# A hybrid S5 and attention layer on one core: the norm of x on VectorE, a pinned order from the u products on, the keys' norms a tile behind, and block 0's output matrices and lags behind the keys

## The chip, the cores and the metric

The kernel runs on one core of a Trainium2 chip. The metric is the device time of one execution in microseconds, shown as the median of three runs. Five engines work at the same time, each through its own queue in order: TensorE (PE in the profile; PEld is its weight load), VectorE (DVE), ScalarE (ACT), GpSimd (POOL) and SyncE (SP), which issues all the transfers here. Engines wait for one another by semaphores.

## What is computed

One layer of a diffusion backbone, on 512 latent tokens x and 256 context tokens ctx of width 1024, conditioned by a vector c. Cut to what the change touches:

```
mod    = silu(c) @ w_mod + b_mod            # 6 vectors of 1024; another set from c_ctx for ctx
h      = rmsnorm(x, norm1)   * (1 + sc1)  + sh1
hc     = rmsnorm(ctx, norm1) * (1 + csc1) + csh1
q, k, v, u, g = split(h @ w_in)             # ctx: k, v, u alone
k      = rope(rmsnorm(k));  kc = rmsnorm(kc)     # two key heads of 128
y      = s5(u, uc)                          # scan over the tokens, both directions, 32 groups of 64 complex states
attn   = softmax(q [kc, k]^T / sqrt(128)) [vc, v]
x      = x + g1 * ((sig(ga) * (attn @ w_ab) + sig(gs) * glu(gelu(y))) @ w_out)
x      = x + g2 * conv_ffn(rmsnorm(x, norm2) * (1 + sc2) + sh2);  out = rmsnorm(x)
```

The S5 scan is worked in chunks of 8 tokens: input matrices W (from B and powers of the step A), output matrices H (from C), the products inside a chunk ("lags", from H, C and W), and a scan over the chunks.

## The kernel before, in words

Every matrix product takes three TensorE products (`mm3`, L129), because weights and activations are split into a high and a low part: ScalarE casts the high part, and the low part is the remainder, by GpSimd for weights (`split`, L134, L136) and by VectorE for activations. Weights come through three staging buffers `wr` and two pairs `wh`, `wl` (`weight`, L138). PSUM has four single banks ("a") and two double ones ("s").

The head of the program, in the order of the code:

1. Constants, x, the first modulation weights (`load_wm`, two buffers in each of two tags, 1 MB each for one of eight tiles) and ctx are asked for on SP. VectorE and ScalarE work out the S5 step: sines, powers, the tables `ws`, `hs`, `wa`, `wb` (L244 to L329).
2. `rstd_first` (L350): for x, ScalarE squares each of eight tiles and TensorE adds up all eight with a product by ones; for ctx, VectorE adds the squares and TensorE multiplies only the sum and the last square. Then logarithm and exponential give the reciprocal root.
3. For each of eight tiles k (L408): the modulation sums of tile k+1 (`mod_sums`: eight products with a 32-column left side, a copy of the row by VectorE), the turning of tile k's row into columns (`mod_turn`, `finish`), then h for x and ctx (scaling on VectorE L416, shift on ScalarE L417, remainder on VectorE L418), and the u products: `ul` (latent, 512 wide) and `uc` (context, 256 wide), 12 of each.
4. u goes to DRAM and back in another layout (`ub`, `ud`, `us`). `s5_build(0)` makes W, the padded copies of it on ScalarE (L493), and H on VectorE, twelve passes of 128x1024.
5. `keys` (L660): for two heads, a tile for ctx and one for the latents: 24 products `kp`, ScalarE's square, a ones product `kss` for the sum, rotary products on VectorE, reciprocal root, scaling, split.
6. `s5_lags(0)`: products `kps`, a copy and a correction on VectorE, a store to DRAM and eight loads back as `tp`. `turn` makes the rotation tables of a half block.
7. The S5 stage (L785): four blocks in two halves. `weave` interleaves VectorE's `s5_half` with TensorE's steps; `filler` hands out value tiles `vp`, gates `proj` and the rest of the modulation in small pieces, so TensorE has work while VectorE scans. `s5_out` closes a half.

What sets the order: the framework schedules instructions by their dependences and its own estimate of times; `nosync` adds an order without a wait. From L783 on (`pinned[0] = True`) each TensorE instruction is tied behind the one before it in the code; ahead of it the scheduler mixes tiles as it sees fit. `behind` (L229, L418) holds the S5 products `tt` back behind the latest remainder of h.

Of the kernel before, what the change touches and what calls it, by code (L numbers as in the profile page):

```python
# [18 lines left out]
KT = 8  # L19
L = 512  # L20
# [9 lines left out]
LOADS = "xxwcw"  # L30
WU_V = ()
PO2 = 2
GAP, F0, F1, F2, F3, WM = 2, 8, 13, 5, 2, 2
PO3 = 0
# [28 lines left out]
def hybrid_layer_kernel(ctx: ExitStack, tc: tile.TileContext, io, out):  # L63
# [56 lines left out]
    def pe(ins):  # L120

        if pinned[0]:
            nosync(ins, last[0])
        last[0] = ins
# [67 lines left out]
    x = [None] * 8  # L192
    cx = k8("y8", [KT, LC])
    i = 0
    for what in LOADS:
        if what == "x":
            xt = k8("x8", [4, L])
            S.dma_start(xt, io["x"][:, 4 * i:4 * i + 4])
            x[4 * i:4 * i + 4] = [xt[:, j] for j in range(4)]
            i += 1  # L200
        elif what == "c":
            S.dma_start(cx, io["ctx"])
            S.dma_start(sd, io["sd"])
        else:
            load_wm()
# [23 lines left out]
    behind = [None]  # L229

    def tt(o, a, b, op, eng=V):
        i = eng.tensor_tensor(o, a, b, op=op).ins  # L232
        if behind[0] is not None:
            nosync(i, behind[0])
# [17 lines left out]
    z1, z2, ang8 = sm("n"), sm("n2"), sm("a8")  # L252
    r1, r8 = sm("r1"), sm("r8")
    wrap(ang, r1, z1)
    V.tensor_scalar(r1, r1, PI_LO, -PI_LO, op0=OP.min, op1=OP.max)
    table("silu_and_others")
    sn, co, ab = sm("sn"), sm("co"), sm("ab")
    act(sn, r1, AF.Sin)
    A.activation(ab, r1, AF.Abs)
    act(co, ab, AF.Sin, scale=-1.0, bias=half_pi)  # L260
    V.tensor_scalar(ang8, ang, float(TC), None, op0=OP.mult)
    wrap(ang8, r8, z2)
    fr, fhi, flo = sm("fr"), sm("fhi"), sm("flo")
    V.tensor_scalar(fr, r8, 1.0 / TWO_PI, None, op0=OP.mult)
    V.tensor_scalar(fhi, fr, 192.0, None, op0=OP.add)
    V.tensor_scalar(fhi, fhi, 192.0, None, op0=OP.subtract)
    tt(flo, fr, fhi, OP.subtract)

    pw = tz([8, 2, 32], "tab", 2)
    pf = tz([8, 2, 32], "tab", 2)  # L270
    tt(pw[:, 0, 0], mag, co, OP.mult)
    tt(pw[:, 0, 1], mag, sn, OP.mult)

    def cmul(o, a, b, n):

        c1, c2 = tz([8, 32], "bb", 2)[:, 0:n], tz([8, 32], "bb", 2)[:, 0:n]
        br, bi = (b[:, None, i].to_broadcast([128, n, 32]) for i in range(2))
        tt(c1, a[:, :, 0], br, OP.mult)
        tt(c2, a[:, :, 1], bi, OP.mult)
        tt(o[:, :, 0], c1, c2, OP.subtract)  # L280
        tt(c1, a[:, :, 0], bi, OP.mult)
        tt(c2, a[:, :, 1], br, OP.mult)
        tt(o[:, :, 1], c1, c2, OP.add)

    cmul(pw[:, 1:2], pw[:, 0:1], pw[:, 0], 1)
    cmul(pw[:, 2:4], pw[:, 0:2], pw[:, 1], 2)
    cmul(pw[:, 4:8], pw[:, 0:4], pw[:, 3], 4)
    den, nr, c1, c2 = sm("den"), sm("nr"), sm("c1"), sm("c2")
    tt(c1, lr, lr, OP.mult)
    tt(c2, li, li, OP.mult)  # L290
    tt(den, c1, c2, OP.add)
    V.reciprocal(den, den)
    V.tensor_scalar(nr, pw[:, 0, 0], 1.0, None, op0=OP.subtract)
    ni = pw[:, 0, 1]
    tt(c1, nr, lr, OP.mult)
    tt(c2, ni, li, OP.mult)
    tt(c1, c1, c2, OP.add)
    tt(pf[:, 0, 0], c1, den, OP.mult)
    tt(c1, ni, lr, OP.mult)
    tt(c2, nr, li, OP.mult)  # L300
    tt(c1, c1, c2, OP.subtract)
    tt(pf[:, 0, 1], c1, den, OP.mult)
    cmul(pf[:, 1:8], pw[:, 0:7], pf[:, 0], 7)

    ws, hs = tz([2, 32, 8], "ws"), tz([2, 32, 8], "hs")
    for o, i, up in ((ws, pf, 0), (hs, pw, 0)):
# [873 lines left out]
```

## Time and profile before

| what | us |
|---|---|
| median of three runs (978.12 to 981.64) | 979.43 |
| the profiled execution | 978.9 |
| its span, from the first to the last instruction | 976.8 |
| busy in it: TensorE / VectorE / ScalarE / GpSimd | 920.1 / 495.2 / 416.8 / 364.5 |

The mean granted clock of TensorE is 0.977 of its full speed. The span is cut into 40 slices of 24.4 us below; a digit is the busy share of a slice in tenths. The head of the program is the first five slices:

```profile
PE   5897889999978999999999999999999999999996
DVE  6559799595417777777434553433333333200103
ACT  7324644344364445544533443444434444432332
POOL 1124132332323222222246420665555655554552
PEclk9998989999998999999999999999999999999998
```

A busy TensorE is not one at its peak: each matmul is recorded with its latency, and neighbours overlap. The time a product really takes is the distance from its start to the next start. Idle time of an engine that is not the bound costs nothing.

### The profile page before, as it was taken

What the parts mean: (1) busy time and instruction counts of PE and PEld (TensorE: products, weight loads), DVE (VectorE), ACT (ScalarE), POOL (GpSimd) and SP (SyncE); (2) the same over time, 40 slices, a digit from 0 to 9 for tenths busy, and PEclk for the clock granted to TensorE, in tenths of its full rate; (3) what the DMA queues carried; (4) which work ended last, traced back from release to release, by engine and by line L of the source; (5) the groups of instructions that cost most, each with busy time, mean ns of one, the idle gap of its engine ahead of it and who ended that gap; (6) DMA issues with size and microseconds to landing.
All of it is one profiled execution on the core that took longest, in us unless ns stands there. A gap on an engine that the chain in (4) does not pass through costs nothing.

```text
span 976.8 us, 15643 instructions
## 1 busy us (share of the span) xinstructions
PE 920.1 (94%) x6142; PEld 741.7 (76%) x6142; DVE 495.2 (51%) x935; ACT 416.8 (43%) x795; POOL 364.5 (37%) x282
## 2 busy tenths in 40 slices
PE   5897889999978999999999999999999999999996
PEld 2676767676657888888778989888888888888886
DVE  6559799595417777777434553433333333200103
ACT  7324644344364445544533443444434444432332
POOL 1124132332323222222246420665555655554552
PEclk9998989999998999999999999999999999999998
DMA  9616546565522111111124620333233233333332
GB/s 358 227 47 190 151 142 185 168 194 179 168 80 77 39 49 44 44 44 45 44 65 140 204 67 1 108 96 98 87 98 98 86 100 95 88 102 93 97 108 87
DMA packets 56377, 107.24 MB, mean 110 GB/s; under 512 B 6000, under 2 KB 19056, under 8 KB 54640
## 3 DMA queue, kind: packets, MB, share of 16 engines
q1 hardware_dynamic: 56304, 106.25, 34.7%
q8 instruction: 48, 0.79, 0.3%
q14 instruction: 25, 0.20, 0.1%
HBM read 101.02 MB, written 5.21 MB: 109 GB/s over the span
## 4 chain that ended last, share of the span: by engine, by line
PE 73%; DVE 10%; ACT 5%; issue 5%; DMA 2%; POOL 1%; DVEq 0%; ACTq 0%; POOLq 0%
PE up L127 25%; PE down L127 12%; PE proj L127 10%; PE po L127 6%; PE sc L127 3%; PE glu L127 3%; PE pab L127 3%; DMA wr<-wo 2%; PE tps L901 2%; PE ul L127 2%; DVE w L232 2%; DVE t L232 2%; DVE k L232 1%; PE kp L127 1%; ACT wh L135 1%
## 5 line engine op out<-in xcount | busy, mean ns | idle before, releaser
L136 POOL TENSOR_TENSOR wl<-wr,wh 128x512 fp32r<-128x512 f32 x226 | 312.3, 1401 | 570.0 <-ACT wh L135 563.2
L127 PE MATMUL up<-t,wh 128*128 128x512 f32 (+1 forms) x768 | 225.2, 377 | 1.1 <-DVE t L1018 1.0
L135 ACT CAST wh<-wr 128x512 fp32r<-128x512 f32 x226 | 128.0, 609 | 119.1 <-PE down L127 40.5
L127 PEld LDWEIGHTS up<-t,wh 128*128 128x128 f32 x768 | 139.9, 188 | 31.3 <-DVE t L1018 2.3
L127 PE MATMUL up<-t,wl 128*128 128x512 f32 (+1 forms) x384 | 144.7, 377 | 0.0
L127 PE MATMUL proj<-h,wh 128*128 128x512 f32 x384 | 141.2, 422 | 0.0
L127 PEld LDWEIGHTS proj<-h,wh 128*128 128x128 f32 x384 | 74.8, 195 | 21.6 <-issue 6.1
L127 PEld LDWEIGHTS up<-t,wl 128*128 128x128 f32 x384 | 72.2, 188 | 14.6
L127 PE MATMUL proj<-h,wl 128*128 128x512 f32 x192 | 77.6, 404 | 2.7 <-POOL wl L136 2.7
L1052 DVE SCALAR_TENSOR_TENSOR zc<-up,pv,zc 128x511 f32<-128x511 f32 x44 | 33.0, 750 | 88.3 <-ACT zc L1051 88.3
L1051 ACT ACTIVATE zc<-up,pv 128x512 f32<-128x512 f32 x44 | 34.2, 777 | 75.0 <-PE up L127 74.9
L1083 DVE SCALAR_TENSOR_TENSOR x<-down,mods,x 128x512 f32<-128x512 f32 (+1 forms) x9 | 6.2, 692 | 91.0 <-PE down L127 91.0
L135 ACT CAST pth<-tps 128x512 fp32r<-128x512 f32 x48 | 28.1, 586 | 47.7 <-PE tps L901 47.5
L127 PEld LDWEIGHTS proj<-h,wl 128*128 128x128 f32 x192 | 37.6, 196 | 8.8 <-POOL wl L136 3.1
L127 PE MATMUL glu<-w,wh 128*128 128x512 f32 x128 | 42.5, 393 | 0.0
L889 DVE TENSOR_REDUCE sc<-sc 128x1 f32<-128x768 f32 x32 | 30.7, 961 | 21.8 <-PE sc L127 21.7
L136 DVE TENSOR_TENSOR ptl<-tps,pth 128x512 fp32r<-128x512 f32 x48 | 33.0, 688 | 13.5 <-ACT pth L135 13.2
L127 PE MATMUL sc<-g,qh 128*128 128x256 f32 (+1 forms) x128 | 36.6, 339 | 0.0
L127 PE MATMUL down<-h,wh 128*128 128x512 f32 x112 | 35.6, 389 | 0.0
L127 PE MATMUL po<-pth,g 128*128 128x512 f32 x96 | 32.9, 423 | 1.0 <-ACT pth L135 0.6
L1053 DVE SCALAR_TENSOR_TENSOR zc<-up,pv,zc 128x511 f32<-128x511 f32 x44 | 33.0, 750 | 1.6
L108 ACT ACTIVATE P<-sc,nb,rq 128x768 f32<-128x768 f32 x32 | 31.9, 997 | 4.1 <-DVE nb L890 2.4
(292 smaller groups left out, 1730.9 us busy)
## 6 DMA issues: line engine op xcount, KB each, us to landing
wr<-wup SPq DMA_DIRECT2D x88, 256.0 KB, 2.7
wm<-wmB SPq DMA_DIRECT2D x32, 512.0 KB, 4.8
wr<-wdn SPq DMA_DIRECT2D x40, 256.0 KB, 2.7
x<-x SPq DMA_DIRECT2D x4, 1024.0 KB, 5.3
g<-wmA SPq DMA_DIRECT2D x4, 1024.0 KB, 8.4
w<-wmA SPq DMA_DIRECT2D x4, 1024.0 KB, 10.1
wr<-wgs SPq DMA_DIRECT2D x16, 256.0 KB, 3.5
wr<-wga SPq DMA_DIRECT2D x16, 256.0 KB, 2.7
```

Source lines behind the costliest of these rows:

```text
L108: i = A.activation(*a, **k).ins
L127: pe(T.matmul(ps, l, r, start=start, stop=stop).ins)
L135: A.copy(hi, src)
L136: eng.tensor_tensor(lo, src, f(hi), op=OP.subtract)
L232: i = eng.tensor_tensor(o, a, b, op=op).ins
L889: V.tensor_reduce(mx, sv, axis=AX.X, op=OP.max)
L901: pe(T.transpose(tps[:, 128 * b:128 * b + 128], Ps[h][b][:, 128 * j:128 * j + 128], ident).ins)
L1051: A.activation(z, ps, AF.Identity, scale=cw[1], bias=pv[:, PV_CB + i:PV_CB + i + 1])
L1052: V.scalar_tensor_tensor(z[:, 1:512], ps[:, 0:511], cw[0], z[:, 1:512], op0=OP.mult, op1=OP.add)
L1053: V.scalar_tensor_tensor(z[:, 0:511], ps[:, 1:512], cw[2], z[:, 0:511], op0=OP.mult, op1=OP.add)
L1083: V.scalar_tensor_tensor(x1[i][:, c], ps[:, c], g2[:, i:i + 1], x1[i][:, c], op0=OP.mult, op1=OP.add)
```

## The change

Its parts:

- **Norm of x.** `rstd_first` always adds the squares on VectorE; TensorE multiplies the sum and the last square. The norm of ctx is moved behind the first tile's u products.
- **S5 step spread.** The table work of step 1 becomes a generator, `discretised`; the entry `DISC[k]` says how many of its pieces are issued with tile k (the last entry, 4, before the norm of x). The tables `wa` and `wb` come last.
- **Order from u on.** TensorE's order is pinned from the start to the end of the u products. In each tile: turn k+1, scale x of k+1 and ctx of k, the latent products of k, the modulation sums of k+2, the context products of k-1. The row of sums is copied by ScalarE, not by VectorE. Loads: both x, then modulation and u weights in turn, ctx after two of the modulation tiles; u weights come in pairs of tiles (`wu` has another layout in DRAM).
- **Keys.** A tile's sum of squares and all behind it (`normed`) is issued inside the next tile's products, after four k of a latent tile or six of a context tile. `keys` yields after each tile, and the rest of `s5_build(0)` (the second half: H, after six steps of W) stands between its two heads.
- **Lags.** `s5_lags(0)` goes from ahead of the S5 stage into its first `weave`, with nine more steps there; the first two steps of `s5_drive(0, 0)` come ahead of the last key's norm.

```
-LOADS = "xxwcw"
+DISC = 1, 2, 2, 2, 2, 2, 2, 0, 4
...
-    rs_x = rstd_first(lambda k: x[k], L, True)
-    rs_c = rstd_first(lambda k: cx[:, k], LC, False)
+    table("silu_and_others")
+    extra = discretised()
+    steps(extra, DISC[KT])
+    table("natural_log_exp_and_others")
+    rs_x = rstd_first(lambda k: x[k], L)
...
+    mod_sums(0)
+    mod_turn(0)
+    scaled(x[0], rs_x, hh[0], 0, 0)
+    low(x[0], hh[0], hl[0], 0, 0)
+    mod_sums(1)
+    for k in range(KT):
+        if k + 1 < KT:
+            mod_turn(k + 1)
+            scaled(x[k + 1], rs_x, hh[k + 1], k + 1, 0)
+            if k:
+                scaled(cx[:, k], rs_c, ch[:, k], k, 1)
+            low(x[k + 1], hh[k + 1], hl[k + 1], k + 1, 0)
+        elif k:
+            scaled(cx[:, k], rs_c, ch[:, k], k, 1)
+        u_of(k, False)
+        if k == 0:
+            rs_c = rstd_first(lambda k: cx[:, k], LC)
+            uc = [bank("uc") for _ in range(2)]
+            scaled(cx[:, 0], rs_c, ch[:, 0], 0, 1)
+        low(cx[:, k], ch[:, k], cl[:, k], k, 1)
+        steps(extra, DISC[k])
+        mod_sums(k + 2)
+        if k:
+            u_of(k - 1, True)
+        if k in (2, 4):
+            wus.append(weight(io["wu"][k // 2 + 1], [2, 512]))
+    u_of(KT - 1, True)
+    run(extra)
+    pinned[0] = False
...
-    run(s5_build(0))
-    behind[0] = None
+    hold[0] = behind[0]
+    first = s5_build(0)
+    steps(first, 6)
+    hold[0] = None
...
     s5_u(0)
-    keys()
-    run(s5_lags(0))
-    run(turn(0))
-    run(turn(1))
+    pinned[0] = True
+    kg = keys()
+    steps(kg, 2)
+    run(first)
+    steps(kg, 2)
...
-    pinned[0] = True
-    run(s5_drive(0, 0))
+    d00 = s5_drive(0, 0)
+    steps(d00, 2)
+    run(kg)
+    run(turn(0))
+    run(turn(1))
+    run(d00)
...
-        weave(s5_half(s, 0), chain(s5_drive(s, 1), fill), 8, 6 + F0)
+        weave(s5_half(s, 0), chain(s5_drive(s, 1), s5_lags(0) if s == 0 else (), fill), 8, 6 + F0 + (9 if s == 0 else 0))
```

**What moves, at three places.** First TensorE from its first instruction to the first u products (`n`: ones products of the norms, `mod`: modulation sums and turnings, `ul`: u products). Before:

```order
L358 MATMUL n_203<-tg,ones 128x512 x8
L127 MATMUL n_231<-p,ones 128x256
L127 MATMUL n_231<-tg,ones 128x256
L378 MATMUL mod<-g_86,cz 32x256 x8
L378 MATMUL mod<-g_90,cz 32x256 x8
L383 MATMUL mod<-cst,bb 32x2 x16
L127 MATMUL ul<-h_263,wh 128x512
```

and now:

```order
L126 MATMUL n_156<-p,ones 128x512
L126 MATMUL n_156<-tg,ones 128x512
L399 MATMUL mod<-g_85,cz 32x256 x8
L404 MATMUL mod<-cst,vr 32x2 x8
L399 MATMUL mod<-g_97,cz 32x256 x8
L404 MATMUL mod<-cst,vr 32x2 x8
L126 MATMUL ul<-h_188,wh 128x512
```

Eight ones products of the norm of x have become two, and the two of the context's norm have gone behind the first tile.

Second TensorE at the end of a head's context keys and the start of its latent ones (`kp`: key products, `kss`: the sum of squares). Before, at the second head:

```order
L127 MATMUL kp<-c_267,wl 128x256
L127 MATMUL kp<-c_268,wh 128x256
L127 MATMUL kss<-tg,ones 128x256
L127 MATMUL kp<-h_263,wh 128x512
L127 MATMUL kp<-h_263,wl 128x512
L127 MATMUL kp<-h_265,wh 128x512
```

and now, within the latent tile of the first head:

```order
L126 MATMUL kp<-h_188,wh 128x512
L126 MATMUL kp<-h_188,wl 128x512
L126 MATMUL kp<-h_190,wh 128x512
L126 MATMUL kss<-tg,ones 128x256
L126 MATMUL kp<-h_189,wh 128x512
L126 MATMUL kp<-h_189,wl 128x512
```

The sum of the context tile, which stood right behind its products, now stands behind twelve products of the next tile.

Third SP at block 0's lags (`ldr`: the store, `tp`: the eight loads back, `wm`: modulation weights, `wr`: staged weights). Before:

```order
L147 DMA wr<-wgs 128x512 x2
L514 DMA ldr<-lg 128x240
L517 DMA tp<-ldr 16x8x128 x8
L732 DMA wm<-wmB 128x1024 x2
L483 DMA bb<-sb 128x256
```

and now:

```order
L531 DMA bb<-sc 128x256
L561 DMA ldr<-lg 128x240
L792 DMA wm<-wmB 128x1024 x2
L564 DMA tp<-ldr 16x8x128 x8
L792 DMA wm<-wmB 128x1024 x2
```

Two modulation loads now stand between the store of the lags and the loads that bring them back.

## Rows read from the trace of the kernel before

**Rows 1.** Windows of core 0, whole head and S5 stage: us, busy by engine, PEclk, DMA share, GB/s:

```profile
0.00:28.43 28.43, 15.00 (x84) 6.82 (x85) 18.63 (x89) 19.94 (x40) 2.63 (x15) 0.94 0.91 346
28.43:76.51 48.08, 45.50 (x384) 35.39 (x385) 28.91 (x53) 14.61 (x27) 13.23 (x9) 0.97 0.35 121
76.51:106.71 30.20, 23.11 (x106) 17.96 (x105) 23.05 (x26) 14.69 (x32) 8.34 (x6) 0.89 0.73 221
106.71:141.00 34.29, 31.36 (x410) 27.44 (x409) 33.44 (x60) 17.69 (x42) 3.90 (x3) 0.95 0.37 106
141.00:283.00 142.00, 134.88 (x1592) 97.10 (x1591) 90.63 (x153) 56.79 (x138) 45.03 (x28) 0.98 0.56 175
```

**Rows 2.** Timeline of TensorE, 0 to 30: start us, us, engine line op, count, idle before and releaser:

```profile
8.65 10.07 PE L358 MATMUL n<-tg,ones 128*128 128x512 f32 x16 [8.65 <-ACT tg L357]
...
23.62 2.52 PE L378 MATMUL mod<-g,cz 128*32 128x256 f32 x32
...
28.43 0.79 PE L127 MATMUL ul<-h,wh 128*128 128x512 f32 x1 [1.43 <-ACT h L417]
```

**Rows 3.** Timeline of ScalarE, 18 to 22:

```profile
18.52 0.62 ACT L309 COPY ws<-tab 128x256 f32<-128x256 f32 x1
...
19.59 0.67 ACT L108 ACTIVATE tp<-n,cc 128x512 f32<-128x512 f32 x1
20.18 1.01 ACT L339 ACTIVATE tg<-y 128x256 f32<-128x256 f32 x3
21.09 0.61 ACT L108 ACTIVATE tp<-tp 128x512 f32<-128x512 f32 x1
```

**Rows 4.** Waits of TensorE to 110 (total, times, longest), and its timeline at 84:

```profile
PE kss L127 <- ACT tg L670: 7.1, 4, 4.5
...
84.04 1.22 PE L127 MATMUL kss<-tg,ones 128*128 128x256 f32 x2 [4.49 <-ACT tg L670]
```

**Rows 5.** Timeline of ScalarE, at 83:

```profile
82.95 0.63 ACT L493 ACTIVATE wpad<-k 64x128 f32<-64x128 f32 x2 [4.53 <-DVE k L232]
```

**Rows 6.** Timeline of VectorE, at 9 and 109:

```profile
8.91 0.35 DVE L232 TENSOR_TENSOR bb<-tab 128x64 f32<-128x64 f32 x2
...
109.36 0.69 DVE L679 TENSOR_TENSOR tg<-tg 128x512 f32<-128x512 f32 x1
```

**Rows 7.** Timelines of VectorE and GpSimd, at 70:

```profile
69.43 1.22 DVE L232 TENSOR_TENSOR k<-bb,ws 128x1024 f32<-128x1024 f32 x1
70.57 2.31 DVE L232 TENSOR_TENSOR t<-bb,ws 128x1024 f32<-128x1024 f32 x1
...
69.99 1.81 POOL L136 TENSOR_TENSOR wl<-wr,wh 128x512 fp32r<-128x512 f32 x1 [8.04 <-ACT wh L135]
```

**Rows 8.** DMA issues to 120: queue, count, KB each, us to landing:

```profile
y<-ctx SPq DMA_DIRECT2D x1, 1024.0 KB, 12.2
```

**Rows 9.** Timeline of TensorE in the u products, 29 to 42:

```profile
29.02 0.63 PE L127 MATMUL ul<-h,wl 128*128 128x512 f32 x1
29.45 0.63 PE L127 MATMUL ul<-h,wh 128*128 128x512 f32 x1
...
37.31 0.39 PE L127 MATMUL ul<-h,wh 128*128 128x512 f32 x1
37.54 0.28 PE L127 MATMUL uc<-c,wh 128*128 128x256 f32 x1
37.65 0.28 PE L127 MATMUL uc<-c,wl 128*128 128x256 f32 x1
...
41.65 0.31 PE L383 MATMUL mod<-cst,bb 128*32 128x2 f32 x16 [0.42 <-DVE bb L390]
41.95 1.07 PE L378 MATMUL mod<-g,cz 128*32 128x256 f32 x16
```

**Rows 10.** Timelines of SP and TensorE, block 0's lags and output, 113 to 127:

```profile
113.32 5.30 SPq L517 DMA_DIRECT2D tp<-ldr  x8
...
126.54 1.58 PE L617 MATMUL gp<-w,tg 64*64 64x128 f32 x32 [2.06 <-DVE tg L232]
```

More of the change, by code (lines that the diff above doesn't have):

```diff
@@ L120, in pe @@
     def pe(ins):
-        if pinned[0]:
+        if pinned[0] and last[0] is not None:
             nosync(ins, last[0])
@@ L190, in load_wm @@
             S.dma_start(wms[k], io["wmA"][k])
-    x = [None] * 8
-    cx = k8("y8", [KT, LC])
[L194 to L205, printed above, removed]
+    x = []
+    for i in range(2):
+        xt = k8("x8", [4, L])
+        S.dma_start(xt, io["x"][:, 4 * i:4 * i + 4])
+        x += [xt[:, j] for j in range(4)]
+    load_wm()
+    wus = [weight(io["wu"][0], [2, 512])]
+    load_wm()
+    cx = k8("y8", [KT, LC])
+    S.dma_start(cx, io["ctx"])
+    S.dma_start(sd, io["sd"])
+    load_wm()
+    wus.append(weight(io["wu"][1], [2, 512]))
+    load_wm()
+    pinned[0] = True
     table("natural_log_exp_and_others")
@@ L263, in hybrid_layer_kernel @@
[L263 to L298, printed above, removed]
@@ L363, in rstd_first, with run, steps @@
         return rs
-    rs_x = rstd_first(lambda k: x[k], L, True)
-    rs_c = rstd_first(lambda k: cx[:, k], LC, False)
+    def run(gen):
+        for _ in gen:
+            pass
+    def steps(gen, n):
+        for _ in range(n):
+            next(gen, None)
+    table("silu_and_others")
[3 more added lines that the diff above has]
+    rs_x = rstd_first(lambda k: x[k], L)
     sc1b = tl([8], "sc1b")
@@ L405, in hybrid_layer_kernel @@
[L405 to L418 removed]
+        V.tensor_scalar(shm[:, k], ps[:, 256:258], pv[:, PV_BMOD + k:PV_BMOD + k + 1], None, op0=OP.add)
@@ new lines, in hybrid_layer_kernel @@
+    ul = [bank2("ul") for _ in range(2)]
+    mod_sums(0)
[24 more added lines that the diff above has]
+            wus.append(weight(io["wu"][k // 2 + 1], [2, 512]))
@@ L443, in s5_u @@
         S.dma_start(us[s], us_[s].rearrange("t (q j) c -> (t q) j c", j=8))
-    def run(gen):
-        for _ in gen:
-            pass
     def weave(one, two, n, m):
@@ L660, in keys, with normed @@
     def keys():
-        table("natural_log_exp_and_others")
+        todo = [None]
+        def normed():
+            if todo[0] is None:
+                return
+            g, n, off, sq, kr = todo[0]
+            todo[0] = None
+            ss = bank("kss")[:, :n]
+            mm(ss, ones, sq[:, :n], True, True)
+            rs = sq[:, :n]
+            rstd_of(ss, n, rs, 1.0 / HD, eps)
+            V.tensor_tensor(kr, kr, rs, op=OP.mult)
+            split(kr, kh[:, g, off:off + n], kl[:, g, off:off + n])
         for g in range(KVH):
@@ L676, in keys @@
                     A.mul(kr, ps, pv[:, PV_QK + 1:PV_QK + 2])
-                rs = sq[:, :n]
-                rstd_of(ss, n, rs, 1.0 / HD, eps)
-                V.tensor_tensor(kr, kr, rs, op=OP.mult)
-                split(kr, kh[:, g, off:off + n], kl[:, g, off:off + n])
+                todo[0] = g, n, off, sq, kr
+                yield
+        normed()
         table("silu_and_others")
+        yield
     s5_u(0)
-    keys()
-    run(s5_lags(0))
-    run(turn(0))
-    run(turn(1))
-    def steps(gen, n):
-        for _ in range(n):
-            next(gen, None)
+    pinned[0] = True
+    kg = keys()
+    steps(kg, 2)
+    run(first)
+    steps(kg, 2)
     def v_tile(j, w):
```

195 lines of the change are left out of this document (115 added, 80 removed).

## The prediction

> **What bounds the kernel now.** I read first the busy time by stage, then TensorE's timeline, then the engines that release it. One core runs; the profiled execution took 978.9 us, its span 976.8, the median of the three runs is 979.43. In [rows 1] the program is cut at five points of TensorE's work: the first u product (28.43), the first key product (76.51), the first lag product (106.71), the end of the value tiles (141) and the end of the S5 stage (283). The reader is to see that TensorE is busy 15.00 of 28.43 us in the first piece, 45.50 of 48.08 in the second, 23.11 of 30.20 in the third, and 31.36 of 34.29 and 134.88 of 142.00 behind. So TensorE sets the pace from the u products on, and what is to be had lies in the first and the third piece, and a little in the second. What comes after 283 the change does not touch.
>
> First piece, [rows 2]: TensorE idles 8.65 us, then spends 10.07 us on eight pairs of ones products for the squares of x, takes the modulation sums only at 23.62, and reaches u at 28.43. In [rows 3] ScalarE carries the matrices of the S5 step, the logarithm and, between it and the exponential at 21.09, three squares of the context. Third piece: TensorE waits four times, 7.1 us together, for the square of the key products [rows 4], the longest 4.49. ScalarE held that square back: ahead of it in its queue stood the padded copies, which had waited 4.53 us for VectorE's first S5 matrix [rows 5]. The clock in that piece is 0.89 [rows 1].
>
> **The change, part by part**
>
> *Norm of x.* Removed from TensorE: sixteen records, 10.07 us [rows 2]; left are four (two ones products). Added on VectorE: six additions of 128x512, 0.69 us each by the like one at 109.36 [rows 6], about 0.6 from start to start. VectorE came to the 128x64 product at 8.91 [rows 6] with some 1.4 us of table work ahead of it that the change moves behind the norm, so I put its first addition at 8.6. Six additions and the small products between them (1.4) end at 13.6, the two ones products (2.5, a quarter of the 10.07) at 16.1. But ScalarE takes the logarithm behind the four copies of the S5 matrices, 0.54 each from start to start [rows 3], and the last pair of these wait for VectorE's remaining 2 us of products, which end at 15.7 at the earliest; the copies then end at 16.8, with semaphores 17.3.
>
> Here the two splits of the first weights on GpSimd fall in the same microseconds. [Rows 7] show the price: a VectorE product of 128x1024 with both inputs in SBUF takes 1.22 us alone and 2.31 us when it overlaps GpSimd's split at 69.99, so about 1.1 us a split. With none in the way the copies end at 17.3, with both at 19.5. I take one, 18.4, since only the second lies fully in that window; both ends stay for the range. The Trainium skill (SBUF — State Buffer, section "Who interferes with whom") says that VectorE with two SBUF inputs and a GpSimd instruction that reads SBUF exclude each other for the whole instruction. By that rule both splits would block, the sum below would lose 1.1 us more, and it speaks against putting the norm on VectorE; rows 7 agree with it.
>
> From 18.4 ScalarE has two passes of 512 for logarithm and exponential, 0.6 each like the one at 21.09, eight of 256 or less at 0.34 like the squares at 20.18 (the copy of the first sums, five squares of the context, a small copy, the copy of the second sums), and h, 0.65 (its scaling on VectorE lies beside the squares). That is 4.6, and 0.5 for the semaphores: u begins at **23.5** instead of 28.43, a gain of 4.9 [rows 2, 3]. The context's squares stand in front of h in ScalarE's queue, so its landing counts: it took 12.2 us from issue to landing [rows 8] with 1 MB of modulation weights ahead of it, now two and the u weights, which puts it near 18.5, no later than ScalarE wants it. The table load that vanishes (1.3 us of ScalarE) lay beside TensorE's sums: nothing. Ends of the term: 1.5 (the context lands 2 us later, both splits block) and 6.5.
>
> *The u products, pinned, the context a tile behind.* Nothing is added; the order is fixed. At full clock a 128x512 product takes 0.23 us from start to start and a 128x256 one 0.11 (37.31, 37.54, 37.65), a modulation sum 1.07, its turning 0.30 [rows 9]. So 96 x 0.34 = 32.6, six sums 6.4, seven turnings 2.1, the context's norm 1.2: 42.3. The first tile runs at half rate (0.43 a product, 29.02 to 29.45), 12 x 0.20 = 2.4, and I allow 1.0 for the first turnings, where the context's logarithm stands before the copy on ScalarE. That is 45.7 against 48.08: **2.4** gained. In each later tile the copy of the sums has a context product (12 x 0.11 = 1.4) to hide behind, and h of the next tile has about 5.5 us. VectorE's first S5 products and the tables (the steps spread over the tiles) fit into its idle time: it is busy 28.91 of 48.08 [rows 1]. On SP the u weights wait for their staging buffers behind GpSimd's splits, and the modulation weights are queued behind them; each is wanted two tiles after it is asked for, over 10 us. Ends: a loss of 1 and a gain of 4.8.
>
> *Keys.* The four sums move 12 or 18 products behind their squares. Two tiles of 24 at 0.11 and two of 24 at 0.23 are 16.3, four ones products about 0.65 each at full clock 2.6 (the one at 84.04 took 1.22 at half rate [rows 4]), so 18.9 against 30.20: **11.3** gained, of which 7.1 are the waits and the rest is the clock and the idle queue behind them. The padded copies still stand ahead of the first square on ScalarE, and VectorE starts the S5 matrix only after the last u remainder; but 2.8 + 2.8 us of TensorE work now cover that square. The last sum stands between block 0's transposes and the first value tile, beside which its logarithm runs. Ends: 8 and 12.5.
>
> *Output matrices and lags of block 0 behind the keys.* The lag products (1.2 us on TensorE) move into the S5 stage; the step boundary moves with them, so they cost nothing more. Nine more steps are woven into the first half, three of lags and six of value tiles, which are taken earlier, not added. The lags' way is new: copy, store, then eight loads that take SP 5.30 us to issue [rows 10], now with two modulation loads ahead of them that wait for TensorE's first modulation product. Between lags and block 0's output TensorE has 84 value products (0.12 each) and two modulation sums, 12.5 us; the lags need about 2.3 + 5.3 + 2.4 = 10 and what VectorE and the queue add. I call that even. In the other direction TensorE no longer meets the 2.06 us wait of that output for VectorE [rows 10]. Term 0, ends a gain of 4 and a loss of 6.
>
> **Sum:** 4.9 + 2.4 + 11.3 + 0 = 18.6. 978.9 - 18.6 = 960.3; the median lies 0.5 above the profiled run, so **961 us**. A measurement of this kernel can tell about 0.3% (3 us) from no change.
>
> **The rivals**
>
> *VectorE becomes the bound.* It is busy 33.44 of 34.29 us from 106.71 on and 23.05 of 30.20 before [rows 1]. If its work on the S5 blocks paces the stage, the gain is only what VectorE can move forward: its S5 work starts at 69.43 [rows 7], in the change when the last u remainder is done, near 64, and 7.2 us of idle time in the third piece. 5.4 + 7.2 = 12.6, so 967. Against it: TensorE waits for VectorE in the S5 stage only 2.06 us.
>
> *The lags come late.* If the eight loads do not get ahead before the modulation loads are done, block 0's output waits up to 8 us (5.3 and the landing): 969. With the one above it would leave nothing measurable: 977 to 982.
>
> *The order costs the clock.* Where TensorE in its fixed order waits in every tile, the granted clock may stay at 1.2 GHz through u. At 0.43 and 0.215 a product u would take 61.9 instead of 32.6 and the sums 6 more: 960 + 35 = 995, slower than before. It decides if the waits for turned sums grow from nothing to about a microsecond a tile and the clock falls with them. For it: the half rate at 29.02 [rows 9] after a stop of 1.43 us [rows 2]. Against it: the piece from 28.43 has a granted clock of 0.97 with 2.6 us of idle time in it [rows 1]. The Trainium skill (TensorE: Matmul & The Clock Gate, section "HAM oscillation — how this bites in real kernels") warns that short groups with waits between them throttle the engine anew each time; the trace shows it in the keys, not in u.
>
> *More than forecast:* the half-clock stretches and waits up to 283 (some 10 us idle in the last two pieces) shrink too: 950.
>
> **How the numbers follow.** Forecast 0.72 (952 to 970 by the ends, not all at once), VectorE or late lags 0.11 (965 to 975), both 0.05 (no change), clock 0.07, more 0.05. Faster by over 0.3%: 0.72 + 0.11 + 0.05 = 0.88; within: 0.05; slower: 0.07. The range 951 to 972 takes in the forecast's ends and most of the second case, leaving out about 0.2.
>
> **What would show it.** In the new profile: first u product near 23.5, first key product near 69, first value product near 89.5 instead of 108.8, waits for the key squares gone, granted clock near 1 in the keys, and the distance from the first value tile to the end as before. Wrong, if u begins after 27, if TensorE waits at each turning, if block 0's output waits over 4 us for the lags, or if VectorE runs without gaps and TensorE waits for it behind 110.

## The result and the profile after

Four runs of the changed kernel beside four of the kernel before: 969.24 us against 979.95 (medians), ratio 0.9895, 95% interval 0.9867 to 0.9923. A second, later series (nine runs of it beside 25 of the kernel before) gave 972.14 against 978.57, ratio 0.9934 (0.9912 to 0.9955). So the change saves 0.7 to 1.1%, 6 to 11 us; 18.6 were forecast. The profiled execution took 968.9 us, its span 966.9. The ratios further below leave out one execution each of e1 (1488.74 us) and b2 (1030.09 us), far above all others of the same kernel.

Windows of the changed kernel, cut at the same events as [rows 1] (first u, key and value product, then the first product of the attention's output and the first of the up projection); columns as there:

```profile
0.00:24.53 24.53, 7.30 (x69) 2.71 (x69) 17.35 (x75) 17.57 (x36) 4.00 (x16) 0.93 0.93 360
24.53:71.19 46.66, 46.09 (x388) 34.83 (x389) 39.67 (x69) 18.51 (x38) 14.63 (x7) 0.96 0.40 146
71.19:95.80 24.61, 21.20 (x114) 17.00 (x112) 18.56 (x22) 14.91 (x35) 10.19 (x7) 1.00 0.84 265
95.80:308.76 212.96, 194.44 (x2177) 145.81 (x2177) 145.81 (x267) 94.95 (x213) 56.27 (x38) 0.97 0.48 145
...
308.76:582.43 273.67, 267.50 (x1630) 224.50 (x1629) 169.71 (x351) 122.06 (x228) 81.13 (x56) 0.99 0.23 70
582.43:966.90 384.47, 374.89 (x1760) 308.63 (x1758) 107.72 (x152) 149.54 (x255) 198.46 (x160) 1.00 0.31 91
```

The kernel before between the same events, from the first value product on:

```profile
108.76:321.91 213.15, 194.56 (x2116) 147.16 (x2114) 146.41 (x266) 94.29 (x212) 57.85 (x36) 0.95 0.47 143
...
321.91:594.78 272.87, 267.45 (x1630) 224.83 (x1628) 169.61 (x351) 122.23 (x228) 80.97 (x56) 0.99 0.23 70
594.78:976.80 382.02, 372.48 (x1760) 307.65 (x1758) 106.59 (x152) 149.15 (x255) 199.50 (x160) 0.99 0.31 92
```

The reader is to see: u starts 3.9 us earlier and takes 1.4 less; the first value product comes 13.0 earlier (1.2 of that is the lag products, which moved behind it); the S5 stage is as long as before; the piece behind it takes 0.8 more; and the last piece, which the change does not touch, takes 2.45 us more with the same 1760 products.

**The head.** VectorE, GpSimd and ScalarE of the changed kernel, at 14 to 20:

```profile
13.89 1.36 DVE L232 TENSOR_TENSOR tab<-bb 128x128 f32<-128x128 f32 x1
15.28 1.64 DVE L232 TENSOR_TENSOR bb<-tab 128x224 f32<-128x224 f32 x2
```

```profile
13.74 2.64 POOL L135 TENSOR_TENSOR wl<-wr,wh 128x512 fp32r<-128x512 f32 x2 [11.85 <-ACT wh L134]
```

```profile
18.54 0.64 ACT L323 COPY ws<-tab 128x256 f32<-128x256 f32 x1 [2.08 <-DVE tab L232]
...
19.61 0.68 ACT L107 ACTIVATE tp<-n,cc 128x512 f32<-128x512 f32 x1
```

The like of these two forms take 0.29 and 0.69 where GpSimd is idle (in e3 below). GpSimd's two splits lay there, both blocked VectorE, and ScalarE took the logarithm of [rows 3] only behind the copies, at 19.61. That is no earlier than the 19.59 of the kernel before: what u gains, it gains behind the logarithm.

**The keys.** The waits for the key squares of [rows 4] are gone. In their place, TensorE, then SP and ScalarE of the changed kernel:

```profile
73.50 0.39 PE L126 MATMUL kp<-c,wl 128*128 128x256 f32 x1 [0.53 <-POOL wl L135]
...
87.29 0.49 PE L126 MATMUL kp<-h,wh 128*128 128x512 f32 x1 [2.50 <-ACT g L483]
...
95.80 0.50 PE L126 MATMUL vp<-wh,c 128*128 128x256 f32 x2 [0.39 <-ACT gt L597]
```

```profile
47.52 24.05 SPq L146 DMA_DIRECT2D wr<-wk  x4
73.47 0.33 SPq L146 DMA_DIRECT2D wr<-wv  x1
73.85 0.42 SPq L530 DMA_DIRECT2D bb<-sb  x1
74.38 0.38 SPq L487 DMA_DIRECT2D ud<-g  x1
```

```profile
86.86 0.37 ACT L483 COPY g<-uc 128x256 f32<-128x256 f32 x1 [3.49 <-DMA ud<-g]
```

The first SP row takes in four loads; before the fourth, at 71.25, SP stood 11.8 us, since its staging buffer was in use until GpSimd's split, begun at 66.51, ended at 71.23. The first store of a u tile was queued behind that load, the other stores behind the first. ScalarE's copy of the last u tile waited 3.49 us for a store to free its buffer, that tile held a PSUM bank, and the last key tile waited for the bank.

### The profile page after: what moved, and what is told of

Its sections match the earlier page's. It is cut to its first block, busy times and chain, and to the rows that moved or that the text cites. A ratio compares the mean times of both kernels' runs of the same rounds, so it can differ in the third digit from the quotient of the medians.

```text
span 966.9 us, 15631 instructions
## 1 busy us (share of the span) xinstructions
PE 911.4 (94%) x6130; PEld 733.5 (76%) x6130; DVE 498.8 (52%) x933; ACT 417.5 (43%) x802; POOL 364.7 (38%) x282
## 4 chain that ended last, share of the span: by engine, by line
PE 70%; DVE 12%; issue 6%; ACT 6%; DMA 4%; POOL 2%; DVEq 0%; SPq 0%; POOLq 0%; ACTq 0%
PE up L126 25%; PE down L126 13%; PE proj L126 11%; PE po L126 6%; PE sc L126 4%; PE glu L126 3%; PE pab L126 3%; PE tps L965 2%; DVE p L232 2%; DVE t L232 2%; DMA wr<-wo 2%; DVE w L232 2%; DVE k L232 2%; POOL wl L135 1%; DVE p L634 1%
## 5 line engine op out<-in xcount | busy, mean ns | idle before, releaser
L126 PEld LDWEIGHTS up<-t,wl 128*128 128x128 f32 x384 | 72.3, 188 | 14.8
L1116 DVE SCALAR_TENSOR_TENSOR zc<-up,pv,zc 128x511 f32<-128x511 f32 x44 | 33.0, 750 | 89.8 <-ACT zc L1115 89.8
L134 ACT CAST pth<-tps 128x512 fp32r<-128x512 f32 x48 | 28.2, 586 | 48.1 <-PE tps L965 47.9
L135 DVE TENSOR_TENSOR h<-tg,h 128x512 fp32r<-128x512 f32 x16 | 14.9, 934 | 37.3 <-ACT h L134 37.3
```

The lines of the kernel that those rows point to most:

```text
L126: pe(T.matmul(ps, l, r, start=start, stop=stop).ins)
L134: A.copy(hi, src)
L135: eng.tensor_tensor(lo, src, f(hi), op=OP.subtract)
L1116: V.scalar_tensor_tensor(z[:, 1:512], ps[:, 0:511], cw[0], z[:, 1:512], op0=OP.mult, op1=OP.add)
```

## The experiments

Twelve kernels in three series, each on another chip and beside its own runs of the kernel before (e1 to e4; b1, e5, e6, e8; the change again, b2, e7, e9). The four times are of the profiled execution: first u, key, value product, and first product of the attention's output, which closes the S5 stage.

| run | ratio to before (95%) | u | keys | values | attention |
|---|---|---|---|---|---|
| before | 1 | 28.43 | 76.51 | 108.76 | 321.91 |
| change | 0.9895 (0.9867-0.9923) | 24.53 | 71.19 | 95.80 | 308.76 |
| change again | 0.9934 (0.9912-0.9955) | 23.95 | 71.19 | 95.61 | 319.33 |
| e1 sums at once | 1.0037 (1.0014-1.0061) | 23.88 | 71.49 | 104.36 | 320.23 |
| e2 lags first | 0.9927 (0.9902-0.9953) | 24.25 | 71.22 | 94.89 | 308.89 |
| e3 norm on TensorE | 0.9911 (0.9883-0.9938) | 22.29 | 71.81 | 96.13 | 312.57 |
| e4 no pin | 0.9927 (0.9901-0.9952) | 24.27 | 70.98 | 94.83 | 310.91 |
| b1 delay alone | 1.0010 (0.9992-1.0028) | 28.01 | 76.08 | 106.78 | 320.99 |
| b2 keys' part alone | 1.0020 (0.9999-1.0041) | 29.09 | 77.19 | 105.36 | 326.02 |
| e5 stores on ScalarE | 0.9917 (0.9892-0.9941) | 23.88 | 71.75 | 94.25 | 306.94 |
| e6 copies behind h | 0.9925 (0.9895-0.9955) | 22.82 | 69.26 | 91.70 | 304.40 |
| e7 both mends | 0.9883 (0.9855-0.9911) | 22.79 | 69.22 | 91.71 | 304.12 |
| e8 TensorE +5.1 us | 1.0004 (0.9985-1.0022) | 24.48 | 72.58 | 100.14 | 314.97 |
| e9 VectorE +4.8 us | 0.9964 (0.9938-0.9989) | 24.12 | 71.27 | 93.73 | 322.79 |

**e1, the key sums at once.** `normed()` is called right behind each key tile, and no longer in the middle of the next.

```diff
-                    if k == (3 if off else 5):
-                        normed()
...
                 todo[0] = g, n, off, sq, kr
+                normed()
                 yield
-        normed()
```

> The changed kernel with one part undone: each key tile's sum of squares stands right behind its tile again instead of a tile later. Theory A (the delay is what shortened the keys, and TensorE's gain there reaches the end): TensorE waits for the squares again, some 5 to 7 us together; the first value product comes at 101 to 103 instead of 95.8, and the time is 974 to 976 against 969.2 of the changed kernel. Rival B (the keys are now limited by the stores of the u tiles and by the banks that ScalarE's copies hold, the squares would be hidden behind that): the first value product at 96 to 98, the time 969 to 971. Rival C (VectorE paces the S5 stage, so the keys' length does not reach the end): first value product as in A, but the time within 2 us of 969.2.

The waits came back; waits of TensorE from 70 to 310 in e1, and the longest on its timeline:

```profile
PE kss L126 <- ACT tg L732: 6.5, 4, 3.5
```

```profile
88.46 2.07 PE L126 MATMUL kss<-tg,ones 128*128 128x512 f32 x2 [3.50 <-ACT tg L732]
```

The first value product came at 104.36, later than A's 101 to 103, and the time is no better than that of the kernel before: undoing this one part costs the whole gain, 1.0 to 1.4%, more than the 8.6 us of its own place. That alone looks as if the delay were all of the change.

**b1, the delay alone in the kernel before.** The same `keys()` with the sums a tile later and pinned; everything else as before.

```diff
-    keys()
+    pinned[0] = True
+    run(keys())
+    pinned[0] = False
```

> The kernel before with one part of the change alone: the sums of the key squares a tile later, pinned there; u, the norm of x and the lags as before. Theory A (this part is the whole gain at the end): first key product at 76.5 as before, first value product 8 to 10 us earlier (99 to 101 instead of 108.8), ratio to before 0.988 to 0.991. Theory B (the parts add: 8.6 us from the delay, the remaining 2 from u): ratio 0.991 to 0.994. Rival C (the delay pays only together with VectorE's earlier S5 matrices, since VectorE paces the S5 stage): first value product earlier by 8, but the ratio above 0.996.

No gain (1.0010), and the first value product comes 2.0 us earlier, not 8: A and B are out, and of C the ratio alone came true. The first three sums hardly wait; the last one, with nothing behind its tile but itself and the lags, waits 5.08 (TensorE of b1):

```profile
101.60 2.08 PE L127 MATMUL kss<-tg,ones 128*128 128x512 f32 x2 [5.08 <-ACT tg L685]
```

**b2, everything of the change from the keys on, the head as before.** From the first key product on TensorE's order is row for row that of the changed kernel.

```diff
+    first = s5_build(0)
+    steps(first, 6)
...
+    kg = keys()
+    steps(kg, 2)
+    run(first)
+    steps(kg, 2)
...
+    d00 = s5_drive(0, 0)
+    steps(d00, 2)
+    run(kg)
```

> The kernel before with everything of the change from the keys on (sums a tile later, block 0's transposes between the last key tile and the last sum, lags and output matrices behind) and nothing of it ahead: norm of x and u as before. Theory A (the delay pays only when work stands between the last tile and the last sum; the head's part comes on top): first key product at 76 to 76.5, first value product at 99.5 to 101.5, against 106.8 with the delay alone; ratio 0.992 to 0.996. Rival B (the keys' part pays only if u ends early): first value product after 104, ratio above 0.997. Rival C (the head's part never reaches the end, all is the keys'): ratio 0.989 to 0.992. The stage of the up and down products, 382 us in the kernel before and 384 in the changed one with the same TensorE instructions, tells whether those 2 us belong to the head (382 here) or to the part from the keys on (384).

Again no gain (1.0020): B. The same order that takes 24.6 us in the changed kernel takes 28.2 here. VectorE, then TensorE, of b2:

```profile
74.03 2.31 DVE L232 TENSOR_TENSOR t<-bb,ws 128x1024 f32<-128x1024 f32 x1
76.27 2.32 DVE L232 TENSOR_TENSOR k<-bb,ws 128x1024 f32<-128x1024 f32 x1
...
83.58 1.21 DVE L232 TENSOR_TENSOR k<-k,t 128x1024 f32<-128x1024 f32 x1
```

```profile
84.66 0.70 PE L127 MATMUL kss<-tg,ones 128*128 128x256 f32 x2 [1.70 <-ACT tg L691]
...
93.77 2.08 PE L127 MATMUL kss<-tg,ones 128*128 128x512 f32 x2 [3.51 <-ACT tg L691]
```

VectorE, then GpSimd, of the changed kernel at the same place:

```profile
64.32 1.22 DVE L232 TENSOR_TENSOR k<-bb,ws 128x1024 f32<-128x1024 f32 x1
65.45 1.22 DVE L232 TENSOR_TENSOR t<-bb,ws 128x1024 f32<-128x1024 f32 x1
...
70.59 1.72 DVE L232 TENSOR_TENSOR k<-k,t 128x1024 f32<-128x1024 f32 x1
```

```profile
66.51 11.41 POOL L135 TENSOR_TENSOR wl<-wr,wh 128x512 fp32r<-128x512 f32 x4 [7.51 <-ACT wh L134]
```

In the changed kernel VectorE starts block 0's matrix before the splits of the key weights begin and runs at full speed; the splits are held back (2.85 us each on average instead of 1.27; the first 4.72). That costs TensorE 0.53 at the weights, and by way of the fourth load and the stores it leads to the 2.50 shown above. The matrix is ready at 72.3, 1.1 us behind the first key product, so TensorE no longer waits for the first square. In b2 the splits come first, four of VectorE's products double as in [rows 7], and the matrix is ready at 84.8, 7.6 us behind it. So the delay pays only with the rewritten head, as e1, b1 and b2 show together; that the early matrix is the reason is read from the traces.

**e3, the norm of x on TensorE.**

```diff
+            if n == L:
+                sq = t2(n)
+                A.activation(sq, src(k), AF.Square)
+                pe(T.matmul(ps, ones, sq, start=k == 0, stop=k == KT - 1).ins)
+            else:
-            sum_squares(acc, src(k), k, KT - 1, ps)
+                sum_squares(acc, src(k), k, KT - 1, ps)
```

> The changed kernel with the squares of x summed by eight ones products on TensorE, as before, and nothing else undone. Theory A (the norm on VectorE is what brings u forward): the ones products end near 18.8 instead of 17.8 but they no longer share VectorE with the tables, so the copies of the S5 matrices end near 16 to 17; u starts at 24 to 25.5 against 24.53, so by itself that part is worth 0 to 1 us, and the time is 969 to 970. Rival B (the whole 3.9 us by which u starts earlier come from the norm's place): u starts near 28, the time is 972 to 973. Rival C (the norm on VectorE costs time, since its additions push the tables into GpSimd's splits): u starts at 23 to 24 and the time is 968.

C, further than expected: u starts at 22.29. VectorE and ScalarE of e3:

```profile
10.42 0.29 DVE L232 TENSOR_TENSOR tab<-bb 128x128 f32<-128x128 f32 x1
10.75 0.69 DVE L232 TENSOR_TENSOR bb<-tab 128x224 f32<-128x224 f32 x2
...
12.63 0.39 DVE L232 TENSOR_TENSOR tab<-bb 128x224 f32<-128x224 f32 x1
```

```profile
17.23 0.69 ACT L107 ACTIVATE tp<-n,cc 128x512 f32<-128x512 f32 x1 [0.69 <-PE n L373]
...
29.09 0.62 ACT L134 CAST wh<-wr 128x512 fp32r<-128x512 f32 x1 [4.06 <-DMA wr<-wu]
```

Without the six additions VectorE's tables end at 13.0, ahead of GpSimd's splits, and the logarithm comes 2.4 us earlier. But the gain is lost in u: a cast on ScalarE waits for a weight to land until 29.09, the copy of the modulation sums stands behind it, TensorE waits 2.31 for that, and the first key product comes at 71.81. The ratio is not told apart from the change's.

**e4, no pin from the start.**

```diff
     load_wm()
-    pinned[0] = True
```

> The changed kernel without the pinned order from u on (the order is pinned again from the keys on, as in the change). Theory A (the prediction's 2.4 us are the pin's): TensorE meets waits at the turnings again, the u stage takes 48 to 49 us instead of 46.7, the time is 970.5 to 972. Rival B (the gain in u is that of placing each context tile a tile behind, not of the pin): the u stage stays within 0.6 us of 46.7 and the time within 1.5 us of 969.2.

B: u takes 46.71, 46.66 with the pin, although without it TensorE's order is another (210 of the 388 places differ, tiles are mixed again). So the pin is worth nothing here. How much the u stage gains at all is less sure: in five more profiles whose code differs from the change only behind the u products, if at all (the change again, e1, e2, e8, e9), it takes 46.97 to 48.09, against 48.07 to 48.10 with the old head. The first key product comes 3.9 to 5.3 us earlier than in the kernel before in all of them.

**e2, the lags of block 0 first.**

```diff
+    run(s5_lags(0))
     run(turn(0))
...
-        weave(s5_half(s, 0), chain(s5_drive(s, 1), s5_lags(0) if s == 0 else (), fill), 8, 6 + F0 + (9 if s == 0 else 0))
+        weave(s5_half(s, 0), chain(s5_drive(s, 1), fill), 8, 6 + F0)
```

> The changed kernel with the lags of S5 block 0 put back ahead of that block's work instead of being woven into its first half. Theory A (that move is worth nothing, as in the prediction's sum): within 2 us of 969.2; TensorE's 1.2 us of lag products only change places. Rival B (the move costs: weaving the lags in puts VectorE's and ScalarE's work in a worse order, which is the 3 us wait of the projection near 136): 965 to 967. Rival C (the move gains, since TensorE waited for VectorE's first matrix before it could do the lags): the first value product comes 3 to 5 us later and the time is 972 to 974.

A: the ratio lies between the two of the change, and 308.89 against 308.76 at the attention.

**e5, the stores of the u tiles on ScalarE's queue.**

```diff
-        S.dma_start(ud.rearrange("t p c -> p t c"), ub)
+        A.dma_start(ud.rearrange("t p c -> p t c"), ub)
```

> The changed kernel with the four stores of the u tiles issued on ScalarE's queue instead of SP's, where the first of them stood behind the fourth load of the key weights. Theory A (the 2.5 us wait of the third key tile is that store's lateness, by way of the staging buffer and the bank that ScalarE's copy holds): the wait goes, the first value product comes at 92.5 to 94 instead of 95.8, and the time is 966 to 968. Rival B (VectorE paces the S5 stage): the wait goes, but the time stays within 1.5 us of 969.2. Rival C (ScalarE's own queue is delayed by the issues and by the wait for VectorE's copy of the same tile): the wait moves to the key squares, and the time is 969 to 972.

The wait for the bank is gone, 1.26 for a key square came in its place; the keys take 22.50 instead of 24.61, and the attention starts at 306.94. The runs do not tell the time from the change's.

But the stores' queue is not shown to be the reason. In e8 and e9 below all edits lie behind the last key tile and the stores are on SP as in the change; there, too, the wait is absent, and the first store goes out 1.7 us behind the first key product as in e5, against 3.2 in the change. What differs is the first split. VectorE, GpSimd and TensorE of e9:

```profile
66.66 2.32 DVE L232 TENSOR_TENSOR k<-bb,ws 128x1024 f32<-128x1024 f32 x1
```

```profile
66.58 3.55 POOL L135 TENSOR_TENSOR wl<-wr,wh 128x512 fp32r<-128x512 f32 x2 [7.53 <-ACT wh L134]
```

```profile
83.68 1.12 PE L126 MATMUL kss<-tg,ones 128*128 128x512 f32 x2 [1.25 <-ACT tg L734]
```

In both kernels the split asks 0.08 us before VectorE's third product. In the change it is held until 71.23; in e9 it goes through in 1.32 us, VectorE's product waits instead, the fourth load goes out 3.4 us earlier against the first key product, and the keys take 22.46. So it is in the ten profiles with VectorE's matrix at this place: held in four (change, change again, e1, e3: 4.71 to 4.72), through in six (e2, e5 to e9: 1.31 to 1.32). The wait for the bank, 2.2 to 2.5 us, stands in the three of the four whose sums come a tile later, and in none of the six, where a wait of 1.23 to 1.26 for a key square stands instead.

**e6, the copies of the S5 matrices behind the first h.** A constraint on ScalarE's order alone; `first_h[0]` is the instruction that makes the first h.

```diff
-            A.copy(ov[:, 0], iv[:, 0])
-            A.copy(ov[:, 1], iv[:, 1, :, :, ::-1])
+            nosync(A.copy(ov[:, 0], iv[:, 0]).ins, first_h[0])
+            nosync(A.copy(ov[:, 1], iv[:, 1, :, :, ::-1]).ins, first_h[0])
```

> The changed kernel with ScalarE's four copies of the S5 matrices held behind the first tile of h, so that the logarithm of x's norm does not wait for VectorE's last table products (which ran beside GpSimd's splits and took 2 us more for it). Theory A (that wait is what made u start a microsecond later than forecast, and u's start reaches the first key product): first u product at 22.5 to 23.3 instead of 24.53, first key product at 69.5 to 70 instead of 71.2, the time 967.5 to 968.5. Rival B (the first tiles of u are held by what arrives: u and modulation weights and the context keep the DMA queues busy to 36 us): u starts as in A, but the first key product stays at 71 to 71.5 and the time within 1 us of 969.2.

A: u at 22.82, and the 1.7 us reach the first key product (69.26). The wait for the bank is absent too, but this is again a profile in which the first split went through. In time: 0.9925, not told apart.

**e7, both.**

> The changed kernel with both mends: the stores of the u tiles on ScalarE's queue, and the copies of the S5 matrices behind the first tile of h. Theory A (what the two bring at the first value product, 1.5 and 4.1 us in single looks, reaches the end): first value product at 91 to 93, time 2 to 5 us below the changed kernel's in the same call. Rival B (the two remove the same wait, as the second alone showed no wait for the bank either): first value product as with the copies alone (91.7), no gain over that. Rival C (neither reaches the end, the runs' differences are the clock's): the ratio is that of the changed kernel within 0.2%.

Row for row B (91.71 against 91.70), but in time the best kernel of all: 966.68 us, ratio 0.9883 against 0.9934 of the change in the same series, and the intervals just do not overlap (with that of the first series, 0.9895, they do). In this series it is some 5 us faster than the changed kernel and 12 faster than the kernel before, in six runs. Of the two mends only the copies show a gain in the traces, at u (22.79 and 22.82 against 23.88 to 24.53) and at the first key product (69.22 and 69.26 against 70.98 to 72.58). Why e6, with the same milestones, had the higher median of its six runs stays open.

**e8, e9: probes.** Work that nothing uses, behind the last key tile: 22 products on TensorE; eight additions on VectorE.

```diff
+    for i in range(22):
+        mm(ps, hh[0][:, :128], hh[0], i == 0, i == 21)
```

```diff
+    for i in range(8):
+        V.tensor_tensor(delay, f(hh[0]), f(hh[1]), op=OP.add)
```

> The changed kernel with added work: 22 products of 128x512 (into a bank of their own, used by nothing) between the last key product and the first value product, 22 x 0.23 = 5.1 us of TensorE alone. Theory A (TensorE paces the S5 stage, as the prediction's sum assumes): the time rises by 4.5 to 5.5, to 974 to 975. Rival B (VectorE paces it): VectorE works on during the added products, and the time rises by 0 to 2, to 969 to 971. In between: part of each wait for VectorE and ScalarE behind is taken up.

> The changed kernel with added work on VectorE: eight additions of 128x512 (result used by nothing) behind the last key tile, 8 x 0.6 = 4.8 us, of VectorE alone. With 5.1 us more on TensorE the time had risen by 8 to 10. Theory A (TensorE paces the S5 stage and VectorE has slack there): the time rises by 0 to 1.5 us. Rival B (VectorE paces it): by 4 to 6 us. Rival C (both are paced by each other, since TensorE's order is fixed and VectorE's products come just in time): by 2 to 4.

TensorE's 5.1 us cost 0.7 to 1.1% (7 to 11 us). From the first key product to the attention e8 takes 242.39 us, and e5, e6, e7, in which the first split went through as well, 234.90 to 235.19: the whole 5.1, and some 2 more behind a wait of 2.73 for a modulation load. Nothing of it was hidden, so TensorE paces the stage. VectorE's 4.8 us cost 0.3% against the change in the same series, with intervals that overlap: not settled.

**The change again.**

> The changed kernel itself, once more, so that it stands beside the variants on one chip and in as many runs. Its first four runs gave 0.9895 (0.9867 to 0.9923), while five variants of it that each undo or add a small thing lie at 0.991 to 0.993. If those small things cost nothing: 0.991 to 0.9925 here too. If each of them really costs 1 to 3 us: 0.988 to 0.9905.

0.9934, so the small variants of 0.991 to 0.993 need no cost of their own. And the profiled execution, 978.71 us, the slowest of its nine (966.24 to 978.71), is the find: the same kernel reaches the first value product at the same time (95.61), and then takes 10.8 us more for the S5 stage (223.72 against 212.96). VectorE, GpSimd and TensorE in it:

```profile
121.65 2.09 DVE L634 TENSOR_TENSOR_SCAN p<-sp,p 128x96 f32<-128x96 f32 x8
123.66 2.33 DVE L232 TENSOR_TENSOR t<-bb,hs 128x1024 f32<-128x1024 f32 x2
...
130.87 0.55 DVE L232 TENSOR_TENSOR t<-wa,wb 128x384 f32<-128x384 f32 x1
```

```profile
123.72 11.29 POOL L135 TENSOR_TENSOR wl<-wr,wh 128x512 fp32r<-128x512 f32 x3 [26.58 <-ACT wh L134]
```

```profile
132.59 0.79 PE L126 MATMUL proj<-h,wl 128*128 128x512 f32 x1 [6.78 <-POOL wl L135]
...
133.18 1.05 PE L126 MATMUL proj<-h,wh 128*128 128x512 f32 x2
```

VectorE and GpSimd in the first profile of the change:

```profile
122.36 3.16 DVE L634 TENSOR_TENSOR_SCAN p<-sp,p 128x96 f32<-128x96 f32 x8
125.44 4.46 DVE L232 TENSOR_TENSOR t<-bb,hs 128x1024 f32<-128x1024 f32 x2
```

```profile
124.01 4.80 POOL L135 TENSOR_TENSOR wl<-wr,wh 128x512 fp32r<-128x512 f32 x3 [26.67 <-ACT wh L134]
```

In the one, the split of the first projection's weights asks while VectorE is among its scans, gets in (the scans take 3.16 instead of 2.09) and the two engines alternate. In the other it asks 0.06 us after VectorE has begun the 1024-wide products, and gets nothing until VectorE runs out of work at 131.4: one split of 1.27 us takes 8.81. TensorE, in its fixed order, waits 6.78 for it, goes on at half rate (0.43 a product; granted clock 0.80 from 130 to 150), and VectorE then waits in turn. e9 shows the same (6.3 us), b2 too (5.8). In the profiles with no such wait, or one of up to 3 us, the stage from values to attention took 212 to 217 us; in those three, 221 to 229. The profiled executions of b2 (985.01) and e9 (980.52) are at the upper end of their kernels' runs too (976.74 to 985.01, 970.20 to 981.42).

That one wait is less than half of the difference. TensorE's order is the same in both profiles, so they can be laid side by side, product by product. Counted from the first value product, the second is 0.8 us behind before the split, 9.7 at 140, and 4.9 at 151, since the first profile then has a wait of 3.02 that the second is spared. So the split costs 4.1 (reckoned alike, with the change as the yardstick: 3.8 in e9, where a wait of 4.2 for a modulation load comes first, and 3.3 in b2). The other 5.9 come later, behind waits that both profiles have. TensorE at the largest step, the change first, then the change again:

```profile
217.16 0.31 PE L404 MATMUL mods<-cst,vr 128*32 128x1 f32 x16 [2.62 <-ACT vr L804]
```

```profile
223.57 0.39 PE L404 MATMUL mods<-cst,vr 128*32 128x1 f32 x16 [2.63 <-ACT vr L804]
```

and the windows behind it, with the same 51 products:

```profile
217.00:223.00 6.00, 5.84 (x51) 4.14 (x52) 1.62 (x5) 3.64 (x10) 2.20 (x2) 1.00 0.24 74
```

```profile
223.50:232.20 8.70, 8.63 (x51) 5.61 (x52) 1.53 (x5) 3.64 (x10) 2.50 (x2) 0.63 0.22 66
```

After the same wait the granted clock stays at full in the one and falls to its half level (1.2 GHz) in the other; that costs 2.8 us. The wait that ends at 174 in the first profile (3.21 and 3.71; granted clock 0.71 and 0.55 in the 5.8 and 7.1 us behind it) and the one that ends at 266 (3.96 and 3.97; 0.89 and 0.80 in the 16 and 17 us around it) give 1.7 and 1.1 more. What decides it no run here shows.

## Why the prediction was right or wrong

The direction held. The first series lies in the forecast's range (969.24 in 951 to 972), the second just above it (972.14). The 18.6 us of the forecast are 1.7 times what the first series measured (10.7) and 2.9 times what the second did (6.4).

- **Norm of x, 4.9 forecast:** 3.9 in the profile. One split was taken in VectorE's way, both lay there: the value that the rule of the Trainium skill gave (SBUF — State Buffer, section "Who interferes with whom") was the right one, and the trace agrees with it (1.36 for 0.29, 1.64 for 0.69). The cause was wrong as well, so that the size came near is luck: the logarithm comes at 19.61 as before at 19.59, and e3 shows that the sums on VectorE delay u by 1.6 to 2.2 us (22.29 against 23.88 to 24.53 in the profiles with the change's head). What is left is the other part of the edit, which the sum had not priced by itself: in the new order the modulation sums and the first h come ahead of the context's norm. That it makes up the rest is read from the two traces; no run tried it alone.
- **u products, 2.4:** 1.4 in the profile, 0 to 1.1 in five more, and not the pin's (e4).
- **Keys, 11.3:** 6.4 (32.25 to 24.61, less the 1.2 of lag products that left). This is the step that failed, twice. As a term by itself: "The padded copies still stand ahead of the first square … but 2.8 + 2.8 us of TensorE work now cover that square" holds only if VectorE's matrix is ready in time, and b1 and b2 show that without the new head it is not: the terms were added as if each stood alone, and they do not. And in size, though the matrix was ready: the sum priced GpSimd's splits against VectorE in the head and put them at nothing in the keys, where they meet VectorE's matrix. Where the split is held, the fourth key load, the stores behind it on SP and a PSUM bank come late, and TensorE waits 0.53 and 2.50; where it goes through, TensorE waits 1.25 for a key square, and the term is 8.6 (32.25 to 22.46, less 1.2). The rest, 1.4 to 1.9 us, is the 0.39 ahead of the first value product and longer distances beside the sums and the waits.
- **Output matrices and lags, 0:** e2 agrees, within the 0.25% of its interval. The lags were not late.
- **"The distance from the first value tile to the end as before":** true of the S5 stage in the one profile (213.15 and 212.96), not in the other (223.72). The medians of the runs (969.24 and 972.14) lie between the two profiled executions (968.9 and 978.71).
- **The last piece:** about 2 us are lost in up and down products. All eleven profiles with the new head show 384.2 to 384.5 us, the three with the old one (before, b1, b2) 382.0 to 382.3, with TensorE's instructions the same, row for row. The loss is not one wait: the median distance from one up product to the next is 0.233 to 0.234 us with the new head, 0.231 with the old. It comes with the head's rewriting; how, no run here shows.
- **Rivals:** the clock one fell (0.96 in u). VectorE as the bound fell as a whole (e8; e9 leaves a small part open), but something of it is true: VectorE decides when GpSimd's splits are done. The time for both rivals together, 977 to 982, does not follow from their figures: 967 and 8 us for late lags give 975.

## What to carry to other kernels

Do not add up the terms of a change that moves several engines at once: undoing one part (e1) took away the whole gain, and doing the same part alone (b1), or all from the keys on (b2), gave none. Where VectorE and GpSimd both read SBUF, ask of each split whose turn it is, since the loser's user pays; a gap for GpSimd in VectorE's work, ahead of whatever TensorE waits for, is the thing to try (no run here did). Before an edit is credited with a wait that went away, compare how long the splits took in the two profiles: e5 looked like a cure and e8 and e9, which leave that place alone, show the same. And look in a queue for what stands behind a load that waits for its buffer.

## What was not expected of the hardware

One GpSimd split of 1.27 us was held 8.81 us by an unbroken row of VectorE instructions. The Trainium skill (SBUF — State Buffer, section "Who interferes with whom") says that whoever issues first holds the shared ports for the whole instruction; the rows agree for one instruction, and show besides that VectorE's next one came first again, for a dozen instructions (123.66 to 131.42). In the keys the split and VectorE's products lie at the same distance from one another, within 0.01 us, in ten profiles; GpSimd got its turn in six and was held 4.72 us in four. The code up to there is the same in the change (held, in both profiles) and in e8 and e9 (through), so this turn can differ from one execution to the next.

Executions of one kernel differ by more than the parts under study, and time and granted clock go together: 29 runs of the kernel before in the series of e1 to e4 lie between 973.95 us at a mean clock of 0.982 and 982.24 at 0.976 (correlation -0.86). The changed kernel's two profiles have 0.986 and 0.974; the second has longer stretches at the half level behind the wait for the split, and behind three later waits that the first has too. How many of the executions without a profile had the wait for the split is not known.
